# Weight loads capped at 1024 bytes, and the mix reload ordered behind a product

## The chip, the cores and the metric

The kernel runs on one core of a Trainium2 chip. TensorE (PE) multiplies, VectorE (DVE) and ScalarE (ACT) work elementwise, GpSimd (POOL) does reductions over partitions and issues transfers, SyncE (SP) only issues transfers. Each engine takes its instructions in the order of its own queue and waits there for semaphores. The metric is the device time of one execution in microseconds (us): the median of several runs, compared between kernels that ran on the same chip.

## What is computed

A trunk of two layers on 512 tokens of width 2048. Each layer normalises its input and multiplies it with one wide input projection (2048 x 7696); three branches read slices of it:

```python
h = _rmsnorm(x, norm_g)
proj = h @ w_in                      # 512 x 7696
y_conv = conv3(cv_c * cv_h) * cv_b * silu(cv_g)            # 512 columns
y_sb   = stick_breaking(rms(q), rms(k), v) * silu(sb_g)    # 8 heads of 128
y_gla  = rms(gated_linear_attention(...)) * silu(gl_g)     # 4 heads
mix = concatenate([y_conv, y_sb, y_gla])                   # 512 x 2048
return x + mix @ w_out
```

All in float32. The kernel splits each float32 operand of a large product in two float16 parts, high and low, and adds three products.

## The kernel before

**Weights.** Every projection is cut into groups of GW = 256 columns; a list `specs` holds them in the order of use, 38 for each layer, of which 30 read `w_in` and 8 read `w_out`. For a group, `fetch` (L346 to L360) loads 2048 rows of 256 float32 into a tile `st`, in two halves of 1 MB each: partition p gets eight rows of 256 values, which lie 128 rows apart in DRAM and behind one another in the tile. From the fourth group on GpSimd issues these loads, before that SyncE. `st` has two buffers; the load of group i + 2 is issued when group i is taken. Then ScalarE squares the group (`wmax`, L366), GpSimd reduces over partitions (`wscale`, L380), VectorE forms a scale (L383 to L398), ScalarE writes the high part `wh` (`whi`, L435) and VectorE the low part `wl` (`wlo`, L442). For some groups (`quick`) one step of Strassen's scheme is used instead, with seven products of half the size (`wsums`, L485, L486, and a sum of two quarters by an accumulating GpSimd transfer, L503).

**Products.** `project_cols` (L661 to L678) multiplies a group so that columns lie on partitions, `project_toks` so that tokens do; `project_quick` (L749 to L793) does the same by Strassen's seven products, the last of them with the weights `w7h` and `w7l`. They accumulate in three PSUM banks `psp`.

**The mix.** While a branch is ready, `mixsplit` (L866 to L879) scales it and writes the parts to a DRAM tensor `mixd`, because the SBUF buffers for the whole mix still hold the sums `s` that the quick products read. When the second group of the later convolution (`conv c 1`) has been multiplied, `conv_in(1)` calls `mixload` (L881 to L887). It takes these buffers over as `m` (two tiles, high and low part) and loads the finished columns of `mixd` back: three column ranges for each of two tiles, six transfers on SyncE. After that `mixsplit` writes straight into `m`. `weight_ratio` (L1135 to L1152) brings all columns to one common scale (L1150 on ScalarE, L1151 on VectorE), and the output projection reads `m`.

**Attention beside the convolution.** The last pair of heads (j = 3) is worked off piece by piece by `go()` between the parts of the later convolution: `scores` of a head masks (L1230), takes sigmoids into `za` and `zw` (L1238), scans (L1242), multiplies (L1244), writes the high part (L1247) and the low part (L1248) into `za`, and then transposes both by SyncE into `th` (L1250): four transposes for each head, two of 896 and two of 384 columns. `values` multiplies `th` with v (L1266). `za` has two buffers. In the first layer the next layer's small conversion (`wup`, L911) also takes a `za` buffer.

**What sets the order.** The Tile framework orders the instructions of all engines at build time by a simulated timeline (`schedule_with_timeline_sim=True`), among those that are ready by their place in the program. `order(a, b)` (L190) adds an edge of class `NoSync`: a is placed behind b in that plan, but no semaphore is added. The semaphores come from the tiles that are read and written alone. Each weight group is worked on as `hook`s of the product before it: `squares` behind its first matmul, `parts_of` behind a later one. The output projection starts with `project_toks` (L683 to L685), the later convolution's gate (L836 to L839) and its last projection (L673 to L675) stand before it.

Of the kernel before, what the change touches and what calls it, by code (L numbers as in the profile page):

```python
# [17 lines left out]
P = 128  # L18
# [25 lines left out]
def hybrid_trunk(ctx, tc, x, norm_g, w_in, conv_w, conv_b, sb_qn_g, sb_kn_g,  # L44
                 gla_w_up, gla_b_up, gla_on_g, w_out, out):
    nc = tc.nc
# [4 lines left out]
    NT = seq // P  # L51
    HK = KT // 2
    GW = 256
# [17 lines left out]
    def nm(s):  # L71
        uid[0] += 1
        return f"{s}_{uid[0]}"

    def sm(n, tag, bufs=None):
        return small.tile([P, n], F32, tag=tag, name=nm(tag), bufs=bufs or 1 + (tag in TWICE))

    def wk(shape, tag, bufs=None, dt=F32):
        return work.tile(shape, dt, tag=tag, name=nm(tag), bufs=bufs)
# [4 lines left out]
    def bank(pool, tag):  # L84
        return pool.tile([P, 512], F32, tag=tag, name=nm("ps" + tag))
# [104 lines left out]
    def order(a, b):  # L190
        tc.add_manual_dep(a.ins, b.ins.name, mybir.DependencyInfo(
            mybir.DependencyClass.NoSync, mybir.DependencyReason.DATA), reason="order")
# [153 lines left out]
    def fetch(i):  # L346

        l, src, cols = specs[i]
        queue = nc.gpsimd if i > 2 else nc.sync
        staged[i] = st = []  # L350
        whole[i] = stage.tile([P, KT, GW], F32, tag="st", name=nm("st"))
        for h in range(2):
            s_ = whole[i][:, h * HK:(h + 1) * HK, :]
            c0 = cols[0][0]
            queue.dma_start(s_, src[l, h * HK * P:(h + 1) * HK * P, c0:c0 + GW].rearrange("(k p) n -> p k n", p=P))  # L355
            st.append(s_)
        if len(cols) > 1:
            c0, w = cols[1]
            narrow[i] = wk([P, KT, w], "kT")
            nc.sync.dma_start(narrow[i], src[l, :, c0:c0 + w].rearrange("(k p) n -> p k n", p=P))  # L360
# [66 lines left out]
        else:  # L427
            V.tensor_scalar(wh[:, ks, :GW], staged[0][h][:, ks, :GW], scales[0], None, ALU.mult)

    hooks = []  # L430

    def whi(i, h):
        wh = wpool.tile([P, HK, GX], F16, tag="wh", name=nm("wh"))
# [32 lines left out]
    def hook(mm):  # L466

        if hooks:
            hooks.pop(0)(mm)
# [45 lines left out]
    def weights():  # L515

        i = cursor[0]
        cursor[0] += 1
        if i + 2 < len(specs):
            with tc.high_priority():  # L520
                fetch(i + 2)
        assert not hooks
        if i and i + 1 < len(specs):
            hooks.extend([lambda mm: squares(i + 1, mm), lambda mm: parts_of(i + 1, mm)])
        return loaded.pop(i)

    fetch(0)
    for t in range(1, NT):
        xload(t)
    fetch(1)  # L530
    for dst, ap in rows:
        nc.sync.dma_start(dst, ap)
# [60 lines left out]
    def halves(tag, side):  # L593

        return [newbig(tag, [P, NT, KT, P], F16, side) for _ in range(2)]

    mix = halves("x", 0)
    mixd = [dram.tile([P, 2 * NT, KT, P], F16, tag=f"mixd{l}", name=f"mixd{l}") for l in range(depth)]
# [58 lines left out]
    for l in range(depth):  # L657
# [3 lines left out]
        def project_cols():  # L661

            w, u = weights()
            ps = [bank(psp, "p") for _ in range(2)]
            for h in range(2):
                wh, wl = w[h]
                for c, o in enumerate(ps):
                    cs = slice(c * P, (c + 1) * P)
                    for kk in range(HK):
                        k = h * HK + kk  # L670
                        st_ = (h == 0 and kk == 0)
                        en = (h == 1 and kk == HK - 1)
                        T.matmul(o, wh[:, kk, cs], xh[:, :, k, :], start=st_, stop=False)  # L673
                        T.matmul(o, wh[:, kk, cs], xl[:, :, k, :], start=False, stop=False)  # L674
                        mm = T.matmul(o, wl[:, kk, cs], xh[:, :, k, :], start=False, stop=en)  # L675
                        if not h and not c and kk in (0, HK - 1):
                            hook(mm)
            return ps, u  # L678

        def tok_mm(o, ah, al, w, t, k, n, st_, en):  # L680
# [68 lines left out]
        def project_quick(src, sums, y, cols):  # L749

            (w11, wT2, wT3, w22, w21, wt1, wT4), u = weights()
            (pa, pd), (pb, pf) = ([bk[:, n * GW:(n + 1) * GW] for n in range(2)]
                                  for bk in [bank(psp, "p") for _ in range(2)])
            a11, a12, a22 = ([a[:, 2 * r:2 * r + 2, c::2, :] for a in src] for r, c in ((0, 0), (0, 1), (1, 1)))
            s_, a21_22, a12_s, a11_21 = sums

            def prod(o, w, a, start, stop=False):
                for t in range(1 if cols else 2):
                    for kk in range(HK):
                        for i, (p_, q_) in enumerate(((0, 0), (0, 1), (1, 0))):  # L760
                            st_ = start and t == kk == i == 0
                            en = stop and kk == HK - 1 and i == 2
                            if cols:
                                mm = T.matmul(o, w[q_][:, kk, :], a[p_][:, :, kk, :], start=st_, stop=en,  # L764
                                              skip_group_check=True)
                            else:
                                mm = T.matmul(o[:, t * P:(t + 1) * P], a[p_][:, t, kk, :], w[q_][:, kk, :], start=st_,  # L767
                                              stop=en, skip_group_check=True)
                            if start and t == kk == 0 and i == 2 and o is pa:
                                hook(mm)  # L770
                return mm

            y11, y12, y21, y22 = (
                y[:, c, r * GW:(r + 1) * GW] if cols else y[:, 2 * r:2 * r + 2, c * P:(c + 1) * P]
                for r in range(2) for c in range(2))
            za, zb, zd, zf = (a if cols else a.rearrange("p (t c) -> p t c", c=P) for a in (pa, pb, pd, pf))
            prod(pa, w11, a11, True)
            S.activation(y12, za, AF.Copy)  # L778
            hook(prod(pb, wT2, s_, True))
            V.tensor_tensor(y21, zb, y12, ALU.subtract)  # L780
            prod(pd, wT3, a11_21, False)
            S.activation(y22, zd, AF.Copy)
            prod(pf, w22, a12_s, False)
            prod(pa, w21, a12, False)
            S.activation(y11, za, AF.Copy)
            prod(pb, wt1, a21_22, False, True)
            V.tensor_tensor(y12, zb, y12, ALU.subtract)
            V.tensor_tensor(y22, y12, y22, ALU.subtract)
            V.tensor_tensor(y12, zf, y12, ALU.add)
            yield 0, u  # L790
            prod(pd, wT4, a22, False, True)
            V.tensor_tensor(y21, zd, y21, ALU.subtract)
            yield 2, u  # L793

        def project(cols, dst):

            if cursor[0] not in quick:
                return project_cols() if cols else project_toks(xh, xl)
            y = dst()
            for _, u in project_quick((xh, xl), insums, y, cols):  # L800
                pass
            if cols:
                return [y[:, c, :] for c in range(2)], u
            return [y[:, 2 * b:2 * b + 2, :].rearrange("p a c -> p (a c)") for b in range(2)], u
# [52 lines left out]
        def mixscale(j, m, tag, top=11.0):  # L857

            pow2(pmix[:, j:j + 1], m, -top, tag)
            s_ = sm(1, tag + "smix")  # L860
            V.reciprocal(s_, pmix[:, j:j + 1])
            return s_

        mix = []
# [16 lines left out]
        def mixload():  # L881

            mix.extend(halves("m", 1 - l))
            for ks in (slice(0, 2), slice(4, 10), slice(12, KT)):
                assert all(k in split for k in range(ks.start, ks.stop))
                for i in range(2):
                    nc.sync.dma_start(mix[i][:, :, ks, :], mixd[l][:, i * NT:(i + 1) * NT, ks, :])  # L887

# [73 lines left out]
        for tag in ("qT", "kT"):  # L964
# [10 lines left out]
            s_ = sm(1, tag + "s")  # L975
# [42 lines left out]
        for p in range(2):  # L1018
# [52 lines left out]
            for two, bias in ((0, (nT[:, p, 0:1], None, nT[:, p, 2:3], None)),  # L1071
                              (1, (nT01[:, p:p + 1], nT[:, p, 1:2], None, nT[:, p, 2:3]))):
                e = wk([P, 2, 256], "e")
                n = [0, 0]
# [201 lines left out]
        for j in range(4):  # L1276
# [17 lines left out]
            s_ = mixscale(2 + j, m, "b", 12.0)  # L1294
# [138 lines left out]
```

## Time and profile before

| | us |
|---|---|
| median of 3 runs | 1730.08 |
| lowest and highest run | 1726.42 and 1731.79 |
| the profiled execution | 1730.14 |
| its span in the trace | 1728.3 |
| TensorE busy in it | 1661.5 |
| VectorE busy | 1397.8 |
| ScalarE busy | 1177.1 |
| GpSimd busy | 257.8 |

The median is what the prediction is compared with. The rest is from the one profiled execution: its span runs from the first to the last recorded instruction, and all times "at 655" are us from the start of that span. A row of a time-ordered view gives start, duration, engine, line of the kernel, operation, tile written and tile read; in brackets stands the idle time of the engine before it and what ended that idle time. Engine names with a q (SPq, POOLq) are queue entries such as the issue of a transfer. The granted clock is the share of full speed that TensorE's clock had in a stretch.

### The profile page before, as it was taken

The page shows a single profiled execution, that of the slowest core. Times are in us where ns is not written, and L with a number is a line of the kernel's source. Part 1 is how long each engine was busy: PE and PEld are TensorE (multiplying, and loading weights), DVE is VectorE, ACT ScalarE, POOL GpSimd, SP SyncE. Part 2 cuts the span into 40 slices and gives each one's busy share as a digit, 9 for nine tenths or more (in the row PEclk, how much of TensorE's full clock was granted, in tenths as well). Part 3 has the DMA queues.
Part 4 walks back from the last instruction along what each step waited for, and adds up shares of the span by engine and source line. Part 5 has one row for each costly group of instructions (what it writes and reads, how often), then busy time and mean ns, then how long its engine had stood idle before and what let it go on. Part 6 is the DMA issues. An engine that isn't in the chain of part 4 may idle for free.

```text
span 1728.3 us, 39586 instructions
## 1 busy us (share of the span) xinstructions
PE 1661.5 (96%) x16938; PEld 1323.8 (77%) x16938; DVE 1397.8 (81%) x2321; ACT 1177.1 (68%) x1747; POOL 257.8 (15%) x296
## 2 busy tenths in 40 slices
PE   7999999898999999999989999998999899999999
PEld 5744548888989886689976455588898889858998
DVE  7975889879797987687589668898888889878883
ACT  7666677767676785566755676777676867856662
POOL 1211111111212121011111111112111122111010
PEclk9999999999999999999999999999999999999999
DMA  7232324467776877354652223436667777793441
GB/s 250 83 113 98 98 63 114 110 134 139 153 148 148 154 160 221 102 158 144 213 128 98 98 98 98 123 80 143 133 142 144 131 148 134 163 241 115 165 153 50
DMA packets 191889, 232.67 MB, mean 135 GB/s; under 512 B 94354, under 2 KB 152028, under 8 KB 191200
## 3 DMA queue, kind: packets, MB, share of 16 engines
q0 software_dynamic: 70752, 174.08, 37.2%
q1 hardware_dynamic: 111952, 46.61, 14.1%
q10 hardware_dynamic: 9008, 9.45, 1.6%
q8 instruction: 132, 2.16, 0.5%
q14 instruction: 45, 0.37, 0.1%
HBM read 179.65 MB, written 14.68 MB: 112 GB/s over the span
## 4 chain that ended last, share of the span: by engine, by line
PE 37%; DVE 9%; DMA 4%; ACT 3%; issue 2%; POOL 0%; ACTq 0%; SPq 0%; DVEq 0%; POOLq 0%
PE psp L767 13%; PE psp L814 4%; PE psp L673 3%; PE psp L674 3%; PE psp L675 3%; PE psp L685 3%; PE psp L683 3%; PE psp L684 3%; DVE wl L486 2%; DMA th<-za 2%; PE psp L764 1%; ACT junk L366 1%; ACT wh L485 1%; DVE za L1242 1%; DMA st<-st 1%
## 5 line engine op out<-in xcount | busy, mean ns | idle before, releaser
L485 ACT ACTIVATE wh<-st,ws 128x1024 f16<-128x1024 f32 x210 | 234.2, 1144 | 134.6 <-DVE st L506 42.1
L366 ACT ACTIVATE junk<-st 128x2048 uint8<-128x2048 f32 x150 | 285.2, 1901 | 11.8 <-DMA m<-mixd 7.9
L486 DVE SCALAR_TENSOR_TENSOR wl<-st,ws,wh 128x1024 f16<-128x1024 f32 x210 | 266.9, 1280 | 30.5 <-ACT wh L485 30.1
L442 DVE SCALAR_TENSOR_TENSOR wl<-st,ws,wh 128x2048 f16<-128x2048 f32 x82 | 192.0, 2348 | 63.0 <-ACT wh L435 62.7
L767 PE MATMUL psp<-wh,s 128*128 128x128 f16 x2048 | 190.1, 225 | 24.8 <-ACT raw L778 19.5
L767 PEld LDWEIGHTS <-s 128*128 128x128 f16 x3072 | 184.7, 101 | 32.1 <-issue 25.8
L435 ACT ACTIVATE wh<-st,ws 128x2048 f16<-128x2048 f32 x80 | 159.0, 1998 | 66.8 <-DVE ws L396 34.1
L684 PE MATMUL psp<-wl,m 128*128 128x256 f16 x704 | 193.1, 274 | 2.1 <-DVE wl L442 2.1
L683 PE MATMUL psp<-wh,m 128*128 128x256 f16 x704 | 193.0, 274 | 1.3 <-ACT wh L435 1.3
L685 PE MATMUL psp<-wh,m 128*128 128x256 f16 x704 | 193.2, 274 | 0.0
L767 PE MATMUL psp<-wl,s 128*128 128x128 f16 x1024 | 184.2, 225 | 5.0 <-DVE wl L486 4.7
L355 POOL DMA_DIRECT2D st<-in_w_in_dram x114 | 102.4, 903 | 398.1 <-DVE wl L442 286.1
L380 POOL PARTITION_ALL_REDUCE wgm<-wm x75 | 44.0, 587 | 653.6 <-ACT junk L366 624.9
L764 PE MATMUL psp<-s,wh 128*128 128x256 f16 x768 | 131.6, 273 | 2.4 <-ACT qT L778 1.7
L675 PE MATMUL psp<-x,wl 128*128 128x512 f16 x320 | 122.1, 381 | 2.2 <-DVE zun L186 2.2
L764 PEld LDWEIGHTS <-wh 128*128 128x128 f16 x1152 | 112.7, 98 | 14.8 <-issue 1.6
L767 PEld LDWEIGHTS <-m 128*128 128x128 f16 x2160 | 122.6, 98 | 0.5 <-issue 0.3
L673 PE MATMUL psp<-m,wh 128*128 128x512 f16 x320 | 121.3, 379 | 0.8 <-DVE g L839 0.8
L674 PE MATMUL psp<-x,wh 128*128 128x512 f16 x320 | 121.9, 381 | 0.0
L673 PE MATMUL psp<-x,wh 128*128 128x512 f16 x320 | 121.8, 381 | 0.0
L675 PEld LDWEIGHTS <-wl 128*128 128x128 f16 x640 | 62.7, 98 | 76.8 <-DVE wl L442 2.7
L675 PE MATMUL psp<-m,wl 128*128 128x512 f16 x320 | 121.3, 379 | 0.0
(437 smaller groups left out, 4107.5 us busy)
## 6 DMA issues: line engine op xcount, KB each, us to landing
st<-in_w_in_dram POOLq DMA_DIRECT2D x114, 1024.0 KB, 8.3
st<-in_w_out_dram POOLq DMA_DIRECT2D x32, 1024.0 KB, 8.2
st<-st POOLq DMA_DIRECT2D x28, 512.0 KB, 7.3
st<-in_w_in_dram SPq DMA_DIRECT2D x6, 1024.0 KB, 11.7
mixd<-g POOLq DMA_DIRECT2D x24, 256.0 KB, 5.5
x<-in_x_dram SPq DMA_DIRECT2D x4, 1024.0 KB, 4.8
qT<-in_x_dram ACTq DMA_DIRECT2D x8, 512.0 KB, 3.8
qT<-xs ACTq DMA_DIRECT2D x8, 512.0 KB, 5.2
```

Source lines behind the costliest of these rows:

```text
L366: sq = S.activation(junk(HK * GW).rearrange("p (k n) -> p k n", k=HK), staged[i][h], AF.Square, accum_out=peak[i][:, h:h + 1])
L442: V.scalar_tensor_tensor(wl[:, :, :GW], staged[i][h], scales[i], wh[:, :, :GW], ALU.mult, ALU.subtract)
L485: hi = S.activation(h_, b, AF.Copy, scale=sc)
L486: V.scalar_tensor_tensor(l_, b, sc, h_, ALU.mult, ALU.subtract)
L673: T.matmul(o, wh[:, kk, cs], xh[:, :, k, :], start=st_, stop=False)
L674: T.matmul(o, wh[:, kk, cs], xl[:, :, k, :], start=False, stop=False)
L675: mm = T.matmul(o, wl[:, kk, cs], xh[:, :, k, :], start=False, stop=en)
L683: T.matmul(o, ah[:, t, k, :], wh[:, kk, :n], start=st_, stop=False, skip_group_check=True)
L684: T.matmul(o, ah[:, t, k, :], wl[:, kk, :n], start=False, stop=False, skip_group_check=True)
L685: return T.matmul(o, al[:, t, k, :], wh[:, kk, :n], start=False, stop=en, skip_group_check=True)
L764: mm = T.matmul(o, w[q_][:, kk, :], a[p_][:, :, kk, :], start=st_, stop=en, skip_group_check=True)
L767: mm = T.matmul(o[:, t * P:(t + 1) * P], a[p_][:, t, kk, :], w[q_][:, kk, :], start=st_, stop=en, skip_group_check=True)
```

## The change

Two edits. The two loads of a weight group in `fetch` get `max_dma_last_dim=1024`, which caps the contiguous last dimension of a transfer at 1024 bytes; longer ones are split. And the six transfers of `mixload` get an `order` edge behind the last matmul of the projection before, which `project_cols` and `project_quick` now note in `lastmm`: at that call it is the last matmul of the second group of the later convolution, with the weights `w7h`.

```diff
-            queue.dma_start(s_, src[l, h * HK * P:(h + 1) * HK * P, c0:c0 + GW].rearrange("(k p) n -> p k n", p=P))
+            queue.dma_start(s_, src[l, h * HK * P:(h + 1) * HK * P, c0:c0 + GW].rearrange("(k p) n -> p k n", p=P),
+                            max_dma_last_dim=1024)
...
-    hooks = []
+    hooks, lastmm = [], [None]
...
                         if not h and not c and kk in (0, HK - 1):
                             hook(mm)
+            lastmm[0] = mm
             return ps, u
...
             yield 0, u
-            prod(pd, wT4, a22, False, True)
+            lastmm[0] = prod(pd, wT4, a22, False, True)
...
             for ks in (slice(0, 2), slice(4, 10), slice(12, KT)):
                 assert all(k in split for k in range(ks.start, ks.stop))
                 for i in range(2):
-                    nc.sync.dma_start(mix[i][:, :, ks, :], mixd[l][:, i * NT:(i + 1) * NT, ks, :])
+                    order(nc.sync.dma_start(mix[i][:, :, ks, :], mixd[l][:, i * NT:(i + 1) * NT, ks, :]), lastmm[0])
```

## Prediction

> **What bounds the kernel now.** I read the profile from the engine that ends last downwards: the busy shares, then TensorE's list of waits, then a table of short stretches around the later convolution of the first layer, then the queues of SyncE, ScalarE and VectorE there.
>
> ```profile
> PE 1661.5 (96%) x16938; PEld 1323.8 (77%) x16938; DVE 1397.8 (81%) x2321; ACT 1177.1 (68%) x1747; POOL 257.8 (15%) x296
> ```
>
> TensorE is busy for 96% of the span of 1728.3 us, so only about 67 us can be won without removing matmuls, and only where TensorE itself stands still. The list of its waits (us in total, times, longest) says how much of that a transfer or its consequences can be blamed for:
>
> ```profile
> PE psp L814 <- DMA m<-raw: 5.0, 1, 5.0
> PE psz L1226 <- DMA kT<-qp: 4.4, 2, 2.9
> ...
> PE psp L673 <- DVE g L839: 0.8, 1, 0.8
> ```
>
> The largest stall that hangs on the place of the change stands not under DMA but under the makers of weight parts, at the first matmuls of the output projection of layer 0 (TensorE's order of time; in brackets the idle time before a row and its releaser):
>
> ```profile
> 709.24 0.27 PE L683 MATMUL psp<-wh,m 128*128 128x256 f16 x1 [1.31 <-ACT wh L435]
> 711.62 0.37 PE L684 MATMUL psp<-wl,m 128*128 128x256 f16 x1 [2.12 <-DVE wl L442]
> ```
>
> So TensorE was ready at 707.9. The table of stretches shows what that costs (columns: length, busy time and count of PE, PEld, DVE, ACT, POOL, then granted clock, DMA share, GB/s):
>
> ```profile
> 656.00:680.00 24.00, 24.00 (x142) 13.59 (x141) 14.56 (x21) 8.21 (x10) 2.16 (x3) 1.00 1.06 314
> ...
> 704.00:709.50 5.50, 4.19 (x30) 2.58 (x29) 4.04 (x17) 4.91 (x6) 0.36 (x1) 1.00 0.00 0
> 709.50:711.60 2.10, 0.00 (x1) 0.00 (x0) 2.10 (x2) 2.10 (x3) 0.00 (x0) 0.69 0.00 0
> 711.60:717.10 5.50, 5.48 (x26) 3.78 (x26) 1.85 (x2) 5.50 (x6) 0.00 (x0) 0.50 0.01 3
> 717.10:725.00 7.90, 7.90 (x75) 7.07 (x73) 6.02 (x11) 5.50 (x7) 2.19 (x3) 1.00 0.60 191
> ```
>
> After two gaps of 1.3 and 2.1 us the clock is granted at 0.50 for 5.5 us: 26 matmuls there, where at full clock (75 in 7.9 us, 0.105 us each) they need 2.7 us. So the stall costs 1.3 + 2.1 + 2.8 = 6.2 us. Why were the parts late? The queue of SyncE and the two engines that make the parts:
>
> ```profile
> 653.74 1.58 SPq L887 DMA_DIRECT2D m<-mixd  x3
> 655.41 5.93 SPq L1250 DMA_TRANSPOSE th<-za  x1
> 661.44 3.82 SPq L887 DMA_DIRECT2D m<-mixd  x3
> 665.36 26.77 SPq L1250 DMA_TRANSPOSE th<-za  x7
> ```
>
> ```profile
> 679.41 0.69 ACT L1238 ACTIVATE za<-psz,qz 128x512 f32<-128x512 f32 x1 [10.05 <-DMA th<-za]
> ...
> 700.87 0.41 ACT L911 ACTIVATE za<-ga 16x256 bf16<-16x256 f32 x1 [10.20 <-DMA th<-za]
> ...
> 707.20 1.99 ACT L435 ACTIVATE wh<-st,ws 128x2048 f16<-128x2048 f32 x1
> ```
>
> The six pieces of the mix reload (L887; by the code 2 x 128 x 4 x 12 x 128 float16, 3.1 MB) stand between the four transposes of the last pair's first head. ScalarE, which executes in order, stands until 679.41 for these transposes to release za; then everything of the second head is that much late, and it stands again until 700.87 (L911, the next layer's small conversion, needs the same za). Behind L911 come the squares, the scale and at 707.20 the wh that TensorE wanted at 707.9, and after it wl. In layer 1 there is no next layer and no L911; TensorE's whole loss at that place is the 0.8 us of L673.
>
> **The change, part by part.** *Weight loads capped at 1024 bytes.* A row of such a load is GW = 256 float32 in DRAM, which is 1024 bytes already: on that side the cap cuts nothing. What the trace can say of the size in flight:
>
> ```profile
> q0 software_dynamic: 70752, 174.08, 37.2%
> ...
> st<-in_w_in_dram POOLq DMA_DIRECT2D x114, 1024.0 KB, 8.3
> st<-in_w_out_dram POOLq DMA_DIRECT2D x32, 1024.0 KB, 8.2
> st<-st POOLq DMA_DIRECT2D x28, 512.0 KB, 7.3
> st<-in_w_in_dram SPq DMA_DIRECT2D x6, 1024.0 KB, 11.7
> ```
>
> 146 loads of 1024 KB in packets of 1 KB would be 149,504 packets; GpSimd's queue has 70,752 in all. If the 28 sums move in their rows of 512 bytes (28,672 packets, 14.7 MB), the remaining 159.4 MB lie in 42,080 packets, 3.8 KB each: about four rows to a packet. The destination is one run of 8 KB per partition, but a copy whose source comes in rows of 1 KB needs no longer pieces on the other side, so I take this part at zero, with the same packets as before. Its bounds: at best every wait of TensorE on a transposing transfer goes, 5.0 + 4.4 = 9.4 us and one more stretch of half clock (2.8 us as above), 12.2 us. At worst each load takes as long as the six that SyncE issues (11.7 for 8.3 us, +3.4 us), and GpSimd the 1609 ns of a sum for the 903 of a load:
>
> ```profile
> L355 POOL DMA_DIRECT2D st<-in_w_in_dram x114 | 102.4, 903 | 398.1 <-DVE wl L442 286.1 <-DVE w7l L486 65.2 <-DVE wq L392 33.2
> L503 POOL DMA_DIRECT2D st<-st x28 | 45.1, 1609 | 2.7 <-issue 1.5
>   DMA st<-in_w_in_dram: 2.7, 3
> ```
>
> GpSimd waits 398 us before these issues, so 146 x 0.7 = 103 us more of it hide there; the squares (last row: the readers of the weights, L366) now wait 2.7 us in all for a load, so loads have cover, and a load 3.4 us later would show at few of the 73 pairs; I bound it at three stalls of that size, +10 us.
>
> *The reload behind the last product.* The edge is one of order, without a semaphore: it decides where the planner puts the six reloads in SyncE's queue. The last product of the second group is issued from 665.2 to 667.7 on TensorE:
>
> ```profile
> L764 PE MATMUL psp<-x,w7h x16: 272/273/273, 665.2 to 667.7; 128*128 128x256 f16 x16
> 661.63 0.55 DVE L1248 TENSOR_TENSOR za<-zw,za 128x384 f16<-128x384 f32 x1
> 685.79 2.35 DVE L442 SCALAR_TENSOR_TENSOR wl<-st,ws,wh 128x2048 f16<-128x2048 f32 x1
> 688.05 1.56 DVE L1248 TENSOR_TENSOR za<-zw,za 128x896 f16<-128x896 f32 x2
> 689.52 1.41 DVE L839 SCALAR_TENSOR_TENSOR g<-psp,wu,g 128x512 f32<-128x512 f32 x2
> 688.44 1.78 POOL L355 DMA_DIRECT2D st<-in_w_out_dram  x2 [21.68 <-DVE wl L442]
> ```
>
> All four transposes of the first head are ready before that (the last of their sources ends at 662.2, the first L1248 row). So I expect SyncE's order: four transposes, six reloads, the four transposes of the second head. Nothing else on SyncE is passed, no engine waits on the edge, and no bytes are added. Step by step:
>
> 1. The first head's transposes no longer lie behind 1.5 MB of reload. They carry 0.7 MB and share with one pair of weight loads (2.1 MB): at the 314 GB/s of the first stretch 9 us from 655 on, or, for the last one, about 5 us after 662; I take 667. So ScalarE starts L1238 when it is free, at 679.41 - 10.05 = 669.4. Gain for ScalarE and VectorE: 10 us, none of it on TensorE's path.
> 2. The reload now starts about 663 and moves into the second head. Between 664 and its end 3.1 MB of it, 2.1 of weights and 0.5 of residual are in flight; at 314 GB/s that is 18 us, to 682. Its first readers are the rescalings behind L911: covered.
> 3. VectorE's wl (688.14 now, 8.7 after 679.41) ends about 678; the next weight pair (688.44 now) starts about 678.5, and the second head's last two transposes collide with it as they do now. Now they land 12.4 us after that issue (688.44 to 700.87): 691. By bytes (2.1 MB and 0.7 MB more behind the 682) also 691. So L911 comes about 10 us earlier.
> 4. wh follows L911 by 6.3 us (697 in place of 707.20), the end of wl by 10.7 us (711.6 now, 701.7 then). TensorE wants them at 707.9; up to there it is busy without a gap (24.00 of 24.00 us in the first stretch). Margin: 6 us. The stall and its half clock go: 6.2 us. In layer 1 the 0.8 us go, for L839 comes 10 us earlier.
>
> What is late next: TensorE goes on in the output projection 6 us earlier; VectorE, which makes the sums there, also gets free 6 to 8 us earlier, so the gain is kept to the layer's end. **Sum:** 6.2 + 0.8 = 7.0 us. The profiled execution took 1730.14 us (span 1728.3 and 1.8 around it), the median of the runs 1730.08, so they may be exchanged: 1730.1 - 7.0 = **1723.1 us**.
>
> The Trainium skill, "DMA: Bandwidth & Descriptors", section "Issuing engines are not separate DMA queues", says that all queues end on the same 16 engines, so a moved transfer frees no bandwidth. The trace agrees (share 1.06 at 656 to 680). By that rule alone the second head would pay what the first is spared, and the time would be rival 1's.
>
> **The rivals.**
>
> *1. The wait moves, not the stall: 1730.* The reload lies wholly before the second head's transposes in one queue; for it speaks the DMA share of 1.06. If they land at 697 or later, wh comes again when TensorE already waits: each us from there gives one back, and at 701 all of it. Against it: the byte count of step 3 ends at 691.
>
> *2. Slower: L911 in front of the gate.* The rows that decide it:
>
> ```profile
> 685.40 0.38 PE L673 MATMUL psp<-x,wh 128*128 128x512 f16 x1
> 685.61 0.38 PE L674 MATMUL psp<-x,wh 128*128 128x512 f16 x1
> 686.11 1.25 ACT L836 ACTIVATE g<-psp,wu 128x512 f32<-128x512 f32 x2
> ```
>
> The planner places L911 where its own clock has the transposes landed. Now the gate's activation L836 precedes it, and L839 frees the banks from 689.52 on. If the second head comes 10 us earlier in the plan, L911 can come before L836; then the gate waits for the landing, and with it the bank that the next projection's second column needs. That projection starts at 685.40; its first 24 matmuls, 0.21 to 0.22 us apart, use the free bank to 690.6; L911, half of L836 and half of L839 are 0.4 + 0.6 + 0.7 = 1.7 us. So it decides from a landing at 688.9; every us after costs one. At 691 it costs 2 us, still a gain (1725). At 700.9, where it is now because the same weight pair is in its way, it costs 12.0 us, with the half clock after it 2.8 more: 1723.1 + 14.8 = 1738.
>
> *3. The cap does cut: packets of 1 KB.* Transposes, which take turns with the weights' packets, would land sooner everywhere, up to 12.2 us more gain; half of it gives 1723.1 - 6.1 = 1717. The Trainium skill, "DMA: Bandwidth & Descriptors", section "Queues, rings and completion order", says that an engine changes between queues only after a whole packet, which is why smaller pieces would help the other queue. No row here shows the turns themselves. Against the rival: the rows are 1 KB already.
>
> *4. The change does not do what it says: no new order in SyncE's queue*, since the edge waits for nothing: 1730, together with rival 1.
>
> **How the numbers follow.** Forecast (1721.5 to 1725.5) 0.47; rivals 1 and 4 at 1730 0.24; rival 2 at 1738, with any other new order of the planner that leaves a gap, 0.19; rival 3 0.10. A measurement of this kernel tells about 0.3%, 5.2 us, from no change: the lines are 1724.9 and 1735.3. Of the forecast 0.40 lies below it, with rival 3 that is faster 0.50; the rest of the forecast and rivals 1 and 4 make 0.31 within; slower 0.19. The range leaves out the lower half of rival 3 and the greater part of rival 2, and holds the worse bound of the loads (1723.1 + 10 = 1733): 1715 to 1736.
>
> **What would show it.** SyncE's queue about 655 to 667: four th<-za in a row, then six m<-mixd. L1238 without its 10 us in both layers. L911 about 691. No gap at L683 and L684, and no half clock from 710 to 717. GpSimd's queue again 70,752 packets (rival 3: about 180,000). It is wrong if L911 stands past 697, if it precedes L836, or if TensorE has a new wait above 1 us between 690 and 890.

## The result, and the profile after

| | median of runs, us | runs | ratio to before (95%) |
|---|---|---|---|
| before | 1730.35 | 20 | |
| after | 1723.53 (1716.96 to 1732.06) | 20 | 0.9962 (0.9949 to 0.9975) |

The changed kernel is 6.8 us faster; the forecast was 7.0. Its profiled execution, 1729.54 us, is the third longest of its 20 runs, so the profile tells where time went and the runs tell how much. Line numbers behind the first edit are one higher than before, from the middle of the projections on two higher (L1238 is now L1240, L836 L838, L911 L913, L1150 L1152, L435 L436, L684 L686).

SyncE's queue in the first layer, in the profile of after (start, duration, transfer, count): four transposes of the first head, six reloads, four transposes of the second head, as forecast.

```profile
654.26 8.45 SPq L1252 DMA_TRANSPOSE th<-za  x4
662.88 10.30 SPq L889 DMA_DIRECT2D m<-mixd  x6
673.56 10.66 SPq L1252 DMA_TRANSPOSE th<-za  x4
```

ScalarE from there to the first output group, in the same profile:

```profile
663.20 1.16 ACT L1240 ACTIVATE za<-psz,qz 128x512 f32<-128x512 f32 x2 [0.79 <-DMA th<-za]
...
670.31 0.73 ACT L1240 ACTIVATE za<-psz,qz 128x256 f32<-128x256 f32 x2 [4.91 <-issue]
...
678.10 0.67 ACT L838 ACTIVATE g<-psp,wu 128x512 f32<-128x512 f32 x1
688.76 0.41 ACT L913 ACTIVATE za<-ga 16x256 bf16<-16x256 f32 x1 [9.99 <-DMA th<-za]
...
690.87 0.66 ACT L838 ACTIVATE g<-psp,wu 128x512 f32<-128x512 f32 x1
...
698.29 6.96 ACT L1152 ACTIVATE m<-m,ratio 128x1024 f16<-128x1024 f16 x7 [0.94 <-DVE ratio L1149]
705.15 3.88 ACT L436 ACTIVATE wh<-st,ws 128x2048 f16<-128x2048 f32 x2
```

The 10 us in front of the sigmoids that follow the first head's transposes are 0.8 and 4.9 us now. The trace names no cause for the 4.9, but one of these transposes, issued at 661.52, lands at 670.24, 0.07 us before. The second head has landed at 688.76 where it landed at 700.87. But the twelve microseconds do not reach the weights: wh starts at 705.15, only 2.05 us earlier than the 707.20 of before. The small conversion L913 now stands between the two halves of the gate, and the seven rescalings L1152, of which two stood ahead of wh before, now all stand ahead of it. TensorE at the first output product, and the two stretches that answer to those of before:

```profile
709.58 0.27 PE L686 MATMUL psp<-wl,m 128*128 128x256 f16 x1 [2.12 <-DVE wl L443]
```

```profile
709.50:711.60 2.10, 2.02 (x13) 1.55 (x13) 2.10 (x3) 1.38 (x2) 0.00 (x0) 0.66 0.04 8
711.60:717.10 5.50, 5.50 (x43) 4.56 (x42) 3.66 (x6) 4.46 (x6) 2.18 (x3) 0.82 0.43 144
```

Of the two gaps the first (1.3 us, wh) is gone and the second (2.1 us, wl) is still there; the half clock lasts one step of 3.4 us instead of two (43 matmuls in the second stretch, 26 before). So this profile shows about 3 us of the forecast 6.2 at that place: from the first matmul with w7h (L764, 665.16 in before) to the first one behind the wait on m<-raw (L814, 892.36), with 2278 matmuls between them in both, it takes 224.2 us instead of 227.2. In layer 1 the 0.8 us of the gate's wait is gone. The waits on transposing transfers elsewhere and GpSimd's packets are what they were (columns of the first two: total, times, longest):

```profile
PE psp L816 <- DMA m<-raw: 4.9, 1, 4.9
PE psz L1228 <- DMA kT<-qp: 4.8, 2, 3.0
```

```profile
q0 software_dynamic: 70752, 174.08, 37.4%
```

### The profile page after: what moved, and what is told of

Same layout as the page of the kernel before. It is cut to its first block, busy times and chain, and to the rows that moved or that the text cites. A ratio compares the mean times of both kernels' runs of the same rounds, so it can differ in the third digit from the quotient of the medians.

```text
span 1727.7 us, 39585 instructions
## 1 busy us (share of the span) xinstructions
PE 1660.8 (96%) x16938; PEld 1322.3 (77%) x16938; DVE 1397.4 (81%) x2321; ACT 1177.7 (68%) x1747; POOL 256.7 (15%) x296
## 4 chain that ended last, share of the span: by engine, by line
PE 60%; DVE 21%; ACT 7%; DMA 6%; issue 3%; SPq 2%; POOL 0%; ACTq 0%; DVEq 0%; POOLq 0%
PE psp L769 15%; PE psp L816 6%; PE psp L675 6%; PE psp L676 6%; PE psp L674 6%; DVE wl L487 6%; PE psp L686 5%; PE psp L685 5%; PE psp L687 5%; DMA st<-st 3%; DMA th<-za 2%; ACT junk L367 2%; ACT wh L486 2%; PE psp L766 1%; DVE wl L443 1%
## 5 line engine op out<-in xcount | busy, mean ns | idle before, releaser
L436 ACT ACTIVATE wh<-st,ws 128x2048 f16<-128x2048 f32 x80 | 158.8, 1997 | 68.9 <-DVE ws L397 31.4
L686 PE MATMUL psp<-wl,m 128*128 128x256 f16 x704 | 192.8, 274 | 2.1 <-DVE wl L443 2.1
L766 PEld LDWEIGHTS <-wh 128*128 128x128 f16 x1152 | 112.9, 98 | 15.1 <-issue 1.9
## 6 DMA issues: line engine op xcount, KB each, us to landing
st<-in_w_in_dram SPq DMA_DIRECT2D x6, 1024.0 KB, 11.7
```

The source lines that it names most:

```text
L686: T.matmul(o, ah[:, t, k, :], wl[:, kk, :n], start=False, stop=False, skip_group_check=True)
```

## The experiments

Theory: the gain comes from the new order of SyncE's queue alone, and by way of ScalarE. ScalarE stands twice for about 10 us in the before (for the first head's transposes, then for the second's); with less of that it reaches the weights of the first output group sooner, and TensorE's stall there shrinks. Rivals: the cap does it; layer 1 does it; the transposes of the first head are costly wherever ScalarE stands; the difference is run-to-run scatter.

Beside the ratios I use one sum from each trace, **the loss from 640 to 900 us**: TensorE's idle stretches of more than 0.35 us there, added up, and half of each stretch in which the clock was granted at 0.50 and which begins there. Before it is 12.0 + 6.8 = 18.8 us. The half is an upper bound (last section). The last column is measured directly: us from that matmul with w7h to that one behind the wait on m<-raw (L814; L815 or L816 where edits moved the lines), 2278 matmuls in every run but e9, whose order differs.

| run | ratio to before (95%) | gaps + half clock, 640 to 900 | w7h to L814, us |
|---|---|---|---|
| before | | 12.0 + 6.8 = 18.8 | 227.2 |
| e1, cap alone | 0.9994 (0.9980 to 1.0008) | 11.7 + 3.4 = 15.1 | 227.7 |
| e3, order in layer 1 alone | 0.9985 (0.9970 to 1.0000) | 14.8 + 5.1 = 19.9 | 229.6 |
| after | 0.9962 (0.9949 to 0.9975) | 10.1 + 5.1 = 15.2 | 224.2 |
| e10, order in both layers, no cap | 0.9979 (0.9961 to 0.9996) | 8.6 + 5.1 = 13.7 | 224.4 |
| e2, order in layer 0 alone | 0.9974 (0.9954 to 0.9994) | 6.9 + 3.4 = 10.3 | 220.8 |
| e4, another buffer, no new order | 0.9965 (0.9951 to 0.9979) | 8.3 + 3.4 = 11.7 | 222.5 |
| e5, after with wh ahead | 0.9947 (0.9930 to 0.9964) | 8.7 + 3.4 = 12.1 | 220.8 |
| e6, after with the other buffer | 0.9959 (0.9943 to 0.9975) | 7.9 + 1.7 = 9.6 | 222.3 |
| e7, e5 and e6 | 0.9954 (0.9938 to 0.9971) | 8.0 + 3.4 = 11.4 | 222.1 |
| e8, gate behind the conversion | 1.0015 (1.0003 to 1.0027) | 14.4 + 6.8 = 21.2 | 231.1 |
| e9, loads in half rows | 1.0602 (1.0583 to 1.0621) | 25.7 + 10.2 = 35.9 | |
| e11, e5 without the cap | 0.9973 (0.9956 to 0.9989) | 8.8 + 1.7 = 10.5 | 221.1 |
| e12, reload behind both heads | 0.9942 (0.9921 to 0.9962) | 8.0 + 3.4 = 11.4 | 220.2 |

### e1: the cap alone

```diff
+                            max_dma_last_dim=1024)
```

> Only the first edit: the loads of the weight groups get the cap of 1024 bytes, the reload has no order edge. My theory says that the whole gain comes from the new order of SyncE's queue and nothing from the cap, since a row is 1 KB already: ratio to before 1.000 (0.998 to 1.002), 70,752 packets in GpSimd's queue, ScalarE's stall of 10 us at L1238 as before. Rival (the cap does the work): ratio about 0.996, with about 180,000 packets or with transposing transfers that land sooner. Rival (chance, the two kernels differ by less than their runs scatter): ratio anywhere between 0.996 and 1.002.

Measured: 0.9994, and the queue is the old one:

```profile
q0 software_dynamic: 70752, 174.08, 37.4%
```

On every engine its trace has the instructions of the kernel before, in the same order and with the same shapes. The cap cuts nothing: half of the change does nothing, and rival 3 falls with it.

### e2 and e3: the order in one layer alone

```diff
-    order(nc.sync.dma_start(mix[i]..., mixd[l]...), lastmm[0])
+    [order(d, lastmm[0]) for d in [nc.sync.dma_start(mix[i]..., mixd[l]...)] if l == 0]    # e3: l == 1
```

> Only the second edit, and only in layer 0; the reload of layer 1 stays as it was. My theory says that the gain is made at the first matmuls of layer 0's output projection: 1.3 us of waiting and half of the half clock gone (about 4 us, as in the profile of after), up to 6.2 us if the half clock goes on most runs; ratio 0.9965 to 0.998 (-6 to -3.5 us). Rival (the gain comes from layer 1, where SyncE's order is changed too): ratio 0.9995 to 1.000.

> Only the second edit, and only in layer 1. My theory gives it the 0.8 us of the gate's wait (the projection's matmul that waits for the bank that the gate frees): ratio 0.9990 to 1.000. Rival (layer 1 carries more of the 6.8 us than its one stall): ratio 0.9965 to 0.998, and then the profile must show a second place in layer 1 where TensorE lost time before and does not now.

Measured: layer 0 gives 0.9974, layer 1 gives 0.9985. Of the 1731.65 us of before on that chip that is 4.5 and 2.6 us, together what the change gives. In e2's profile the wait at the first output product is down to half a microsecond, and the clock stays at 1.00:

```profile
709.16 0.27 PE L686 MATMUL psp<-wl,m 128*128 128x256 f16 x1 [0.56 <-DVE wl L443]
```

```profile
709.50:711.60 2.10, 2.10 (x22) 1.88 (x20) 2.10 (x2) 1.79 (x2) 0.00 (x0) 1.00 0.04 8
711.60:717.10 5.50, 5.50 (x53) 4.93 (x51) 3.62 (x8) 4.05 (x6) 2.19 (x3) 1.00 0.50 162
```

E2's wh starts at 704.74 and after's at 705.15, so nearly the same moment; but e2's TensorE came to the product at 708.6 and after's at 707.5. The same order of instructions thus leaves a gap of 0.6 or 2.1 us, as TensorE happens to come later or sooner. In e3 both gaps of before are there, 2.8 and 2.1 us:

```profile
709.46 0.27 PE L685 MATMUL psp<-wh,m 128*128 128x256 f16 x1 [2.76 <-ACT wh L436]
711.84 0.27 PE L686 MATMUL psp<-wl,m 128*128 128x256 f16 x1 [2.12 <-DVE wl L443]
```

So layer 0 carries the greater part, as the theory said. Layer 1's 2.6 us is more than its one wait of TensorE (0.8 us in before, 1.3 in e1), but its interval reaches from 0 to 5.2 us, and the trace of e3 shows no second place in layer 1 where time was won. The traces tell its size: from the first matmul with w7h in layer 1 to the last matmul of the kernel (2341 matmuls further on) it takes 203.0 to 203.6 us in the five with the old order there (before, e1, e2, e4, e8) and 202.1 in each of the eight with the reload moved there (after, e3, e5, e6, e7, e10, e11, e12). So layer 1 is worth 0.9 to 1.5 us, and the rest of e3's 2.6 is scatter.

### e4: the conversion in another buffer, nothing reordered

```diff
-        w3 = wk([LR, 3, 2 * P], "za", dt=BF16)
+        w3 = wk([LR, 3, 2 * P], "zw", dt=BF16)
```

> The kernel before, with no edit of the change, but the next layer's small conversion (L911) takes a zw buffer in place of a za buffer, so ScalarE no longer waits there for the second head's transposes; the first head's transposes stay behind the reload and the 10 us at L1238 stay. My theory says that what the change won is only that ScalarE reaches the squares and the scale of the first output group earlier. Then this does as much without touching the reload: squares at 688.7 and about 693.6, the scale about 697, seven rescalings to 704, wh about 704, wl done about 708.3, so the stall of 3.4 us and its half clock shrink to under 1 us; ratio 0.9965 to 0.998. Rival (the transposes of the first head behind the reload are what costs, wherever ScalarE waits): ratio 1.000, L683 and L684 with their gaps of 1.3 and 2.1 us, because values of the second head or the rescalings come as late as before.

Measured: 0.9965, as much as the change. ScalarE's first wait is there in full, the second is gone, and wh comes 6.7 us sooner than before (3.0 of them because this profile is that much earlier already at L1238, 676.41 against 679.41):

```profile
676.41 0.69 ACT L1238 ACTIVATE za<-psz,qz 128x512 f32<-128x512 f32 x1 [10.80 <-DMA th<-za]
...
693.60 6.96 ACT L1150 ACTIVATE m<-m,ratio 128x1024 f16<-128x1024 f16 x7 [1.11 <-DVE ratio L1147]
700.47 3.88 ACT L435 ACTIVATE wh<-st,ws 128x2048 f16<-128x2048 f32 x2
```

No gap is left at L683 and L684. So the transposes of the first head behind the reload cost TensorE nothing by themselves: ScalarE's first wait may stay if the second goes. Layer 1, which this edit leaves alone, still has its wait on the gate, 1.4 us.

### e5: wh ahead of the rescalings

```diff
+            order(S.activation(mix[0][:, :, ks, :], ..., scale=rt_[:, j:j + 1]), his[-1])   # his: the wh of each half
```

The rescaling loop of `weight_ratio` moves behind the projection for this, since an edge points back.

> The changed kernel, and ScalarE's seven rescalings of the mix are ordered behind the two high parts wh of the first output group (VectorE's rescalings are left where they are). In the profile of after the rescalings stand from 698.3 to 705.2 and wh behind them, though its scale is done at 698.8. My theory: the step that failed in my prediction is this one alone, so wh comes at 699 and 701, wl ends by 705.5, before TensorE is ready at 707.5, and the 2.1 us and the 1.7 us of half clock that were left go: 3.8 us below after, ratio to before 0.994 (0.9925 to 0.9955). Rival (the rescalings are needed just as early, since the first product reads the mix): a new wait of TensorE on the rescaled mix takes the place, ratio 0.996 as after, or 0.997 and more.

Measured: 0.9947. In its profile wh starts at 699.50, the rescalings come behind it, and no gap is left:

```profile
699.50 3.90 ACT L436 ACTIVATE wh<-st,ws 128x2048 f16<-128x2048 f32 x2 [1.52 <-DVE ws L397]
703.30 6.94 ACT L1152 ACTIVATE m<-m,ratio 128x1024 f16<-128x1024 f16 x7
```

TensorE does not wait for the later rescalings. To move the seven rescalings is thus enough to remove the 2.1 us that were left in after. That the runs of this version are faster than those of after is not settled: see e11.

### e6 and e7: after, with the other buffer, and with both

```diff
-        w3 = wk([LR, 3, 2 * P], "za", dt=BF16)
+        w3 = wk([LR, 3, 2 * P], "zw", dt=BF16)      # e6: this on the changed kernel; e7: this and e5's edit
```

> The changed kernel, and the next layer's small conversion takes a zw buffer in place of a za buffer, so ScalarE does not stand 10 us before it. My theory: the changed order of the queue and this edit buy the same thing twice, an earlier start of the squares of the first output group. With both, wh comes long before 707.5 and the stall at the first output product goes wholly, but no more than that stall is there to be won: ratio to before 0.994 (0.9925 to 0.9965), 0 to 4 us below after. Rival (the two gains add up, -6.8 from the order and -7 from the buffer): ratio 0.992 or less.

> The changed kernel with both edits of the two runs before: the small conversion in a zw buffer, and wh ahead of the rescalings. My theory: once TensorE does not wait at the first output product there is nothing left for the second edit; ratio as the better of the two, 0.994 (0.9925 to 0.9965). Rival (ScalarE's and VectorE's time behind that product still counts): 0.992 or less, or above 0.9965 if the later rescalings collide with the next group's parts.

Measured: 0.9959 and 0.9954. The two gains of 7 and 6 us, by the order and by the buffer, do not add up: they buy the same stall. Neither profile has a gap at the first output product, and in the last column both lie with e4, 2 us below after. Whether the runs lie below those of after by up to 4 us, as I expected, or not at all, these intervals do not tell.

### e8: rival 2's case on the kernel before

```diff
+            w3a = S.activation(w3[:, i, :], wup, AF.Copy); [order(gates[-1], w3a) for _ in range(l * (i == 0))]
```

The edge puts the second half of the gate of layer 0 behind the first small conversion.

> The kernel before, with one order edge that makes the case of my rival 2: the second activation of the later convolution's gate stands behind the small conversion that waits for the second head's transposes, which land about 700 as in before. By rival 2 the projection after the gate runs out of banks at 690.6 and stands 10 to 12 us; of this 6.2 us come back, because TensorE then reaches the first output product later than its weights, and a half clock of about 2.8 us is added: +5 to +9 us, ratio 1.003 to 1.005. The other theory (the gate has slack there, the three banks carry TensorE further): no gap above 2 us between 685 and 705, ratio 0.999 to 1.001.

Measured: 1.0015, 2.6 us slower, between the two expectations (5 to 9 us by rival 2, no change by the other theory). ScalarE does what the edge asks:

```profile
682.15 0.67 ACT L836 ACTIVATE g<-psp,wu 128x512 f32<-128x512 f32 x1
...
697.98 0.42 ACT L911 ACTIVATE za<-ga 16x256 bf16<-16x256 f32 x1 [13.27 <-DMA th<-za]
698.30 0.66 ACT L836 ACTIVATE g<-psp,wu 128x512 f32<-128x512 f32 x1
```

But TensorE runs without a gap until 703.7, 13 us past the 690.6 at which rival 2 saw it stop; then it waits for the rescaled mix, and the clock falls as in before:

```profile
690.00:700.00 10.00, 10.00 (x48) 4.55 (x47) 1.38 (x3) 2.00 (x3) 0.00 (x0) 1.00 0.72 133
```

```profile
707.45 0.40 PE L683 MATMUL psp<-wh,m 128*128 128x256 f16 x1 [3.74 <-ACT m L1150]
```

VectorE frees the bank of the gate's first half by itself, here at 686 (its L839 starts at 685.57), and the projection's second column takes that one. One conversion between the halves thus costs TensorE nothing before 703.7. That one in front of both halves, with a landing as late as here, would stop it at 690.6 is argued and not shown; e12 has conversions there, but an earlier landing.

### e9: a load that is really cut

```diff
+            for c in (0, GW // 2):
+                queue.dma_start(s_[:, :, c:c + GW // 2], src[..., c0 + c:c0 + c + GW // 2].rearrange("(k p) n -> p k n", p=P))
```

> The kernel before, and each load of half a weight group split into two transfers of 128 columns, so that its rows are 512 bytes and its packets must be smaller than now (GpSimd's queue well above 70,752 packets). This is what a cap would do that did cut. It issues 146 more transfers on GpSimd, and the planner may place some instructions elsewhere. My theory: smaller packets are worth nothing here, since TensorE waits on transposing transfers for 9.4 us in all, and twice the packets make each weight load land later; ratio 1.000 to 1.006. Rival 3 of my prediction (transposes take turns with smaller packets and land sooner everywhere): ratio 0.993 to 0.997, and the waits on m<-raw and kT<-qp shorter than 5.0 and 2.9 us.

Measured: 1.0602, far outside both expectations. The packets are not smaller at all:

```profile
q0 software_dynamic: 73088, 174.09, 39.4%
```

38,912 of them hold 4096 bytes in both kernels, as much as eight rows of 512 bytes here and four of 1 KB in before; the 2,336 more hold 4 bytes each. TensorE waits longer on transposing transfers, not shorter:

```profile
PE psm L1267 <- DMA th<-za: 39.4, 7, 8.7
...
PE psp L815 <- DMA m<-raw: 8.1, 1, 8.1
PE psz L1227 <- DMA kT<-qp: 7.2, 4, 3.2
```

So the run does not test what smaller packets would do, and since the planner also placed work of all engines elsewhere, its 6% can't be put down to one cause. A cap below the row was not run; this way of cutting the rows, at least, gave no smaller packets.

### e10 and e11: the order without the cap, and the same with wh ahead

E10 is the second edit alone, e11 is e5 without the cap. Both run the same instructions in the same order as after and as e5.

> Only the second edit, in both layers, without the cap; it also shows once more what the changed kernel's runs look like. My theory: the same as the changed kernel, ratio 0.996 (0.9945 to 0.9975); in the profile the same order of SyncE, ScalarE at L1238 without its 10 us, and of TensorE's loss from 640 to 900 us 3 to 8 us less than before, by how many steps of half clock fall there. Rival (the cap and the edge together make it): ratio 0.998 or more.

> The changed kernel without the cap, with the seven rescalings behind the two wh of the first output group (as in the run where wh was ahead): the version that I take for the best. My theory: 2 to 4 us below the run with the order alone, ratio to before 0.994 (0.993 to 0.9955). Rival (the difference between the two was chance): the same ratio as the order alone, 0.996.

Measured: 0.9979 and 0.9973. The order alone is faster than before again, by less than in the 20 runs of after, and its profile has the same 2.1 us gap:

```profile
708.20 0.28 PE L685 MATMUL psp<-wl,m 128*128 128x256 f16 x1 [2.12 <-DVE wl L442]
```

Here wh ahead is no faster than the order alone. E5 and e11 have the same instructions and give 0.9947 and 0.9973; after and e10 give 0.9962 and 0.9979. Two measurements of one program thus differ by up to 0.0026, 4.5 us, and the 2 to 4 us between the faster versions lie below that. I take e5's advantage over after in the whole time as not shown. At the place itself the traces show it: in the last column e5 and e11 stand at 220.8 and 221.1 us, after and e10 at 224.2 and 224.4. But e2, with after's order in layer 0, has 220.8 too, because its TensorE came later.

### e12: the reload behind both heads

```diff
+                        t_ = nc.sync.dma_start_transpose(th[hh][:, i, 7 * n:7 * n + zw // P, :], part); [order(d, t_) for d in loads[6 * l:]]
```

This stands on the kernel before; `loads` holds the reload's transfers.

> The kernel before, with the six transfers of the reload ordered behind the transposes of both heads, in both layers (SyncE: eight transposes, then six reloads). The planner now puts two of the small conversions in front of both halves of the gate, which is the case of rival 2 in full. My theory: the 3.1 MB that the second head pays in the changed kernel leave its way, so it lands before 686 instead of 688.8, the conversions before the gate cost nothing because TensorE has a bank until 690.6, and the reload still lands ahead of its first reader at about 696; wh stands by 704, so the stall at the first output product goes: ratio 0.9945 to 0.9975. Rival (the weight pair, not the reload, holds the second head up): it lands at 688 or later as in the changed kernel, the gate then stands behind it and the projection after the gate waits up to some us, ratio 0.998 to 1.002; or the rescalings wait for the late reload, with a gap at the first output product above 2 us.

Measured: 0.9942. All eight transposes go first, and the second head lands at 683.30, 5.5 us before after's:

```profile
655.08 26.10 SPq L1250 DMA_TRANSPOSE th<-za  x8
681.35 3.51 SPq L887 DMA_DIRECT2D m<-mixd  x6
```

```profile
683.30 0.42 ACT L911 ACTIVATE za<-ga 16x256 bf16<-16x256 f32 x1 [2.71 <-DMA th<-za]
...
699.64 2.19 ACT L1150 ACTIVATE m<-m,ratio 128x1024 f16<-128x1024 f16 x2 [0.72 <-DMA m<-mixd]
701.73 3.88 ACT L435 ACTIVATE wh<-st,ws 128x2048 f16<-128x2048 f32 x2
```

The reload is now needed as it lands: the sixth rescaling waits 0.7 us for it. Nothing is left of the stall. Two of the small conversions (683.30 and 685.39) stand in front of both halves of the gate here, which is rival 2's order in full, and TensorE still does not wait at the gate: the landing comes before the 688.9 from which rival 2 counts a cost. Its price for a late landing thus stays untested. The ratio is the best of all (medians 1720.41 against 1730.82 us), with an interval that overlaps those of after, e5 and e7.

## Why the prediction was right, and where it was not

**The cap at nothing**: right. Packets and program are unchanged, and e1 measures 0.9994. Rival 3's sentence on packets that take turns stays untried, because nothing here made the packets smaller. That smaller pieces would help the other queue was my conclusion there.

**Step 1, the first head's landing**: right in kind; I said the transposes land at about 667 and ScalarE starts at 669.4. One of the four landed at 670.24; ScalarE started the first sigmoids at 663.20 and the rest at 670.31. E4 bears out that this gain is not on TensorE's path: there the first wait stays in full and the stall goes.

**Step 2, the reload**: right; the last of the six is issued before 673.2, and the rescalings at 698.29 wait for VectorE's ratio and not for it.

**Step 3, the second head at about 691**: it was 688.76, and 2.3 us of error on a gain of 12 is small. But of its two workings only the count of bytes came near. The weight pair was issued at 682.93 and not at 678.5, and the second head landed 5.8 us behind that issue and not 12.4; with the right moment of issue that working would have given 695. That it also gave 691 was luck. That the reload still lies in the second head's way is shown by e12: with the reload behind it the second head lands at 683.30, 5.5 us sooner. The Trainium skill's rule in "DMA: Bandwidth & Descriptors", section "Issuing engines are not separate DMA queues", that DMAs run on the same 16 engines whoever issues them, agrees with this, but the run does not single it out, because reload and transposes also stand in one queue. The conclusion I drew by that rule alone, rival 1's time, did not come, since the second head gained more than it lost.

**Step 4, wh 6.3 us behind the conversion, at 697**: this step failed. It took the distances behind L911 from the old profile, as if the planner would keep them. The profile of after has 16.4 us between L913 and wh (688.76 to 705.15): the second half of the gate (0.7 us), the load of an activation table (L1354, 1.3 us), both squares (2.1 us each) and all seven rescalings (7.0 us) now stand between them, where before the whole gate, the table load and one square stood ahead of L911 and five rescalings behind the first wh. The margin of 6 us was gone, and 2.1 us of the stall stayed with one step of half clock. E5 moves the rescalings behind wh, and the gap is gone; so their new place by itself was enough to keep it.

**The sum, 7.0 us**: the runs gave 6.8, and in e10, with the same instructions, about 0.2%, 3.6 us (0.0021 of 1729.8). Where the two intervals overlap, 0.9961 to 0.9975, the order is worth 4 to 7 us. The traces say the same more closely. From w7h to L814 it takes 228.2 us in the mean of the three profiles with the old order in layer 0 (before, e1, e3) and 223.1 in the three with the new one (after, e2, e10), about 5 less; the loss from 640 to 900 gives 4.9 (17.9 and 13.1). The three of either kind differ among themselves by 2.4 and 3.6 us, so this is rough. Layer 1 adds 0.9 to 1.5. So the term of layer 0 was 6.2 on paper and is about 5, the sum about 6 to 6.5. The forecast hit the median partly because the scatter of the runs covers the difference.

**Layer 1, 0.8 us**: right; its wait is gone in every profile with the new order there, and the time from w7h to the end is 0.9 to 1.5 us shorter.

**Rival 2**: its order came in part, with L913 between the halves of the gate, but its price was wrong for that order. E8 shows that with the first half in front of the conversion, and its bank freed, the projection behind the gate runs through. In the terms of the prediction, 1738 was worked out for a wait that needs both halves behind the conversion. My remark that it would be wrong if L911 precedes L836 was therefore too strict.

**Rivals 1 and 4**: the order changed, and the stall shrank; both fall.

## What to carry to other kernels

When a stalled in-order engine is released, do not carry its old distances over to the new moment: ask for each instruction behind it what it waits for, because the planner places them anew, and here that put seven rescalings in front of the only one that TensorE wanted. If the same stall hangs on two waits in a row on one engine, look which is cheaper to remove; one buffer name did as much as a reordered queue, and both together did no more. And when versions of a kernel differ by less than two measurements of the same program do (here 0.26%), choose by the trace of the place, from one fixed matmul to another, not by the median.

## What the runs showed of the hardware

**The half clock comes in steps on a grid, and where the grid lies decides what a gap costs.** Every stretch at granted clock 0.50 in these traces is 3.41 us long or a multiple of it, but for the one that runs past the end of the span. Within a run their starts lie on a grid of that length: in before 17.40, 41.29, 78.84 and 334.84 are 7, 11 and 75 steps apart. In another run the grid can lie elsewhere (e2 has 77.92 and 333.92). Counted over all 14 traces from 20 us on, a step of the grid that began at full clock was followed by half clock in all 124 cases in which TensorE stood idle for more than 2.03 us of it, in none of 6,663 with less than 1.83, and in 9 of the 31 between. So a gap of 2.1 to 2.6 us trips the half clock when some 2 us of it fall into one step, and not when the grid cuts it further from its ends. In after the 2.12 us in front of L686 lay wholly in the step from 706.8 to 710.2, and half clock followed; that they lay so was chance.

Up to 640 us the kernel before and e8 run the same instructions in the same order. The first has six such steps there, the second one:

```profile
0.00:640.00 640.00, 609.42 (x6043) 474.28 (x6044) 536.49 (x971) 458.77 (x713) 106.27 (x119) 0.98 0.55 132
```

```profile
0.00:640.00 640.00, 609.09 (x6064) 473.32 (x6065) 540.20 (x976) 462.43 (x718) 105.61 (x119) 1.00 0.55 133
```

The first row is before's, the second e8's (granted clock 0.98 and 1.00). Half of a step, 1.7 us, is the most that it can cost, and these cost less: the first half of the gate (L836) starts at 686.11 in before and at 682.15 in e8, so five steps more came to 4.0 us. That is still more than half of the whole change, between equal instructions; a single profile of after, 1729.54 us, could not have shown the gain of 6.8.

**Rows do not set the packets of GpSimd's loads.** Loads with rows of 1 KB and of 512 bytes both left 38,912 packets of 4096 bytes on GpSimd's queue, and so did the capped load: on the queue the three look alike. The accumulating sums, with rows of 512 bytes, left 28,672 packets of 512.
